# Gates in pairs of block products, heads 0 to 3's operands in the query and key tiles, and norms in three groups, in a decoder layer on one Trainium2 core

## The chip, the cores and the metric

The kernel runs on one core of a Trainium2 chip. The metric is the device time of one execution in microseconds (us); the time shown for a kernel is the median of its runs.

## The reference, cut to what matters

One decoder layer for 1,024 tokens of 1,024 channels, all in float32. A combined projection gives the attention's queries, keys and values, a pooling branch, a memory branch and three sets of gate logits, one set of 1,024 channels for each branch.

```python
h = rms_norm(x, norm_mix_pre)
q_d, k_d, v_d, u_p, q_m, gate_logits = split(h @ w_in)
a = diff_attention(q_d, k_d, v_d, lam)          # 8 heads, two softmax maps each, blocks of queries
a = rms_norm(a, subln_g) * (1.0 - lam_init)     # per head and token, over the head's 128 channels
y_attn = a @ w_attn_branch
...
gates = sigmoid(gate_logits).reshape(B, S, 3, D)
mix = gates[:, :, 0] * y_attn + gates[:, :, 1] * y_pool + gates[:, :, 2] * y_mem
x = x + rms_norm(mix @ w_out, norm_mix_post)
...                                             # then the channel mixer with its up and down products
```

The change concerns the gates of the attention branch (`gates[:, :, 0]`), the attention, its per-head norm and the product with `w_attn_branch`.

## The kernel before, in words

Products run in a split form: `split` writes a float32 tile as a high part (ScalarE, L89) and a low part (VectorE, L90), and `mm3` (L102 to L105) issues three matmuls for each product, high by high, low by high and high by low, in one accumulator of PSUM.

**Gates.** A gate tile `dt` is 128 channels by 1,024 tokens, and there are eight for the attention branch. There are two ways to compute them. `gate(dt)` is a generator that does one tile directly: 8 k-blocks by two halves of the tokens by three matmuls of 128x512, that is 48; it yields after every two k-blocks, so that its pieces can stand between other work, and stores each half from GpSimd's queue to `gate_d` in DRAM. `channels(c0)` does two tiles at once through `seven`: the operands are combined as in Strassen's scheme, with sums of weight pages and sums of the activations that were made once ahead, in seven block products in place of eight. A pair takes 84 matmuls of 128x512 and additions of the seven results on VectorE. The key and query channels go that way, and of the gates tiles 0 and 1.

**Attention.** Heads 0 to 7 run one after another, in four blocks `b` of 256 queries. For a block, `scores` puts two maps in PSUM (`pss`) and makes `z` with a maximum (VectorE) and an exponential (ScalarE); `combine` subtracts the maps with the learned lambda (VectorE, L1184); `turn_weights` transposes `z` on TensorE (`pta`) and splits it to `aT` (L89, L90); `weigh_values` multiplies with the values (`poa`, 24 matmuls of 128x256 and narrower in the last block), copies the result to `ao`, squares it, splits the square and stores `ao` to `ao_d` from GpSimd's queue; `head_norm` sums the squares with a matmul by ones (`pn`) and stores the row to `ss_d`. The steps of a block are issued several blocks apart. `weave(stages, fillers)` writes a head's steps with fillers evenly between: gates 2 and 3 in head 0, the next head's values in heads 0 to 6, its keys (`head_keys`) in heads 1 to 6, gate 4 in head 7. The order on each engine is the order in which the program issues it; `tc.issue_after` moves a step behind another one in the program. Tiles wait for the last user of the bytes that they lie on.

**Norms and merge.** Per-head norms are made in two groups of four heads: `turn_sums(g)` transposes the softmax sums (`ptn`), `load_norms(g)` loads them and the squares from DRAM in a layout with tokens on all partitions, `head_norms(g)` takes the root in small operations on VectorE, and a store puts the factors in `r_d`. Behind the attention, gates 5, 6 and 7 are issued; then for each head the attention's output `a` and its factors `rb` (broadcast to all partitions) are loaded, multiplied (L1384) and split to `ath` and `atl`. `merge_heads(dt, g)` multiplies heads `4g` to `4g + 3` with a page of `w_attn_branch` for output tile `dt`, accumulating in `pya`, and `merge(dt)` applies the gate and adds the other branches. All sixteen tiles of `ath` and `atl` lie in a pool of their own, on bytes that the attention used.

Of the kernel before, what the change touches and what calls it, by code (L numbers as in the profile page):

```python
# [41 lines left out]
def kernel(  # L42
# [818 lines left out]
    with tc.tile_pool(name="gp", reuse_waits="tile", bufs=2, side="right") as gp_:  # L861
# [163 lines left out]

        ss = gp_.tile([P, 4, H4, P], F32, tag="g", name="ss", bufs=3)
# [4 lines left out]
        ready = {2: wsplit(chunk(w_in, C_G + 2 * P), [P, KT, P])}  # L1031
        with tc.issue_after(ready[2][2].ins):
            late[0]()
# [3 lines left out]

    cstack = ExitStack()
    qkp = cstack.enter_context(tc.tile_pool(name="qkp", reuse_waits="tile", bufs=1, side="right"))
    ap_ = cstack.enter_context(tc.tile_pool(name="att", reuse_waits="tile", bufs=3, side="right"))  # L1040
    vpool = cstack.enter_context(tc.tile_pool(name="vp", reuse_waits="tile", bufs=2, side="right"))
# [163 lines left out]
    def weigh_values(h, b):  # L1205
# [10 lines left out]
        for n, ((k, qs, w, ws), i, j) in enumerate(terms):  # L1216
            nc.tensor.matmul(po[:, qs], (vh, vl)[i][:, k, :], w[j][:, ws], start=(n == 0), stop=(n == len(terms) - 1))  # L1217
# [8 lines left out]
        ends["square"] = nc.vector.tensor_tensor(out=sqs[1], in0=sq, in1=sqs[0].bitcast(F32), op=ALU.subtract)  # L1226
# [13 lines left out]
    HG = NH // 2  # L1240
    hns = {}

    def turn_sums(g):

        pt = bank((P, P), "ptn")
        nc.tensor.transpose(pt[0:HG * KT, :], sums[:, g * HG:(g + 1) * HG].rearrange("p h t -> p (h t)"), ident)
        row = ap_.tile([HG * KT, P], F32, tag="trow", name="trow", bufs=1)
        nc.scalar.activation(out=row, in_=pt[0:HG * KT, :], func=AF.Copy)
        nc.sync.dma_start(out=sum_d[g * HG:(g + 1) * HG].rearrange("h (t p) -> (h t) p", p=P), in_=row)

    def load_norms(g):

        st = small.tile([P, 4, HG, 8], F32, tag="hn", name="hn", bufs=1)
        for src, r in ((ss_d, 0), (sum_d, 3)):
            nc.sync.dma_start(out=st[:, r], in_=src[g * HG:(g + 1) * HG].rearrange("h (p f) -> p h f", f=8))
        hns[g] = st

    def head_norms(g):
# [8 lines left out]
        nc.sync.dma_start(out=r_d[g * HG:(g + 1) * HG].rearrange("h (p f) -> p h f", f=8),  # L1267
# [9 lines left out]
    first = gate(2)  # L1277
# [8 lines left out]
    with tc.issue_after(last["load"].ins):  # L1286
        ready[3] = wsplit(chunk(w_in, C_G + 3 * P), [P, KT, P])
        for dt in range(2):
            nc.sync.dma_start(out=gate_d[dt], in_=g01[dt])
    GATES = ((2, 3), (), (), (), (), (), (), (4,))  # L1290
    blocks = [(h, b) for h in range(NH) for b in range(4)]
    for h in range(NH):
        stages = []
        for b in range(4):
# [21 lines left out]
            if h == HG and b == 0:  # L1316
                stages.append(lambda: turn_sums(0))
            if h == HG and b == 1:
                stages.append(lambda: load_norms(0))
            if h == HG and b == 3:  # L1320
                def norms():
                    with tc.issue_after(last["combine"].ins):
                        head_norms(0)
                stages.append(norms)
# [8 lines left out]
        n = 0  # L1333
        for dt in GATES[h]:
            for step in steps(first if dt == 2 else gate(dt), 6 if dt == 2 else 8):
                fillers.insert(min(n, len(fillers)), step)
                n += 2
# [3 lines left out]
    turn_sums(1)  # L1341
# [3 lines left out]
    load_norms(1)  # L1345
# [5 lines left out]
    ath = [atp.tile([P, S], F32R, name="ath%d" % h) for h in range(NH)]  # L1351
    atl = [atp.tile([P, S], F32R, name="atl%d" % h) for h in range(NH)]

    pys = {}

    def merge_heads(dt, g):

        if g == 0:
            pys[dt] = wsplit(chunk(w_attn_branch, dt * P), [P, KT, P])[:2] + (bank(name="pya"), pbank(name="pya"))
        wh, wl, *py = pys[dt]  # L1360
        for i in range(2):
            hs = slice(i * H, (i + 1) * H)
            for k in range(g * HG, (g + 1) * HG):
# [52 lines left out]
    for dt in range(KT):  # L1416
        if dt >= 2:
            merge_heads(dt, 0)
# [379 lines left out]
```

## Time and profile before

| | |
|---|---|
| median of 3 runs | 1728.34 us (1728.09 to 1728.5) |
| profiled execution: its own time, as the profile's span | 1727.6 us |
| TensorE (PE) busy | 1712.8 us, 99% |
| VectorE (DVE) busy | 1241.3 us, 72% |
| ScalarE (ACT) busy | 886.6 us, 51% |
| GpSimd (POOL) busy | 45.0 us, 3% |
| gates 0 and 1 as a pair end | at about 605 us |
| head 0 | 605.8 to 642.1 us |
| heads 1 to 6 | about 33 us each |
| head 7, to the end of its last values | 839 to 882 us |

The profile is one execution; its span is the time from its first to its last instruction. Busy time is the sum of an engine's instructions; PEld is the loading of weights into TensorE, beside its matmuls. A window of the span shows the busy time of each engine in that stretch, which tells where TensorE waits. Lines like L103 are those of the kernel above.

### The profile page before, as it was taken

The numbers are of one execution on the slowest core, as the hardware profiler recorded it, in microseconds if no ns is written. First come the engines' busy times: TensorE is split into PE (matmuls) and PEld (weight loads), VectorE is DVE, ScalarE is ACT, GpSimd is POOL, SyncE is SP. The second block draws the span as 40 slices with busy tenths as digits, with TensorE's granted clock in tenths as the row PEclk, the third lists the DMA queues.
The fourth block names the chain that finished last, engine by engine and source line by source line (L and its number), as shares of the span: only waits on it lengthen the run. The fifth ranks groups of instructions, "written<-read, shape, count | busy, mean of one in ns | idle before, by whom it ended". The sixth has DMA issues, their size and how long they took to land.

```text
span 1727.6 us, 22400 instructions
## 1 busy us (share of the span) xinstructions
PE 1712.8 (99%) x8106; PEld 1421.4 (82%) x8106; DVE 1241.3 (72%) x2047; ACT 886.6 (51%) x1577; POOL 45.0 (3%) x103
## 2 busy tenths in 40 slices
PE   9999999999999999999999999999999999999998
PEld 7888888887888888888888888888888888888886
DVE  6765875666665578888866555848888888878466
ACT  5434544434544467777754344645555555543453
POOL 0000000000000011111110000000000000000000
PEclk9999999999999999999999999999999999999999
DMA  8873544444874686665556571572333423583344
GB/s 273 317 281 114 163 150 133 166 147 143 266 237 159 201 231 170 176 182 152 145 187 239 176 230 50 171 225 92 124 112 107 122 85 98 190 299 106 107 149 142
DMA packets 232803, 294.41 MB, mean 170 GB/s; under 512 B 15865, under 2 KB 161526, under 8 KB 230006
## 3 DMA queue, kind: packets, MB, share of 16 engines
q1 hardware_dynamic: 229158, 285.61, 51.8%
q0 software_dynamic: 3520, 7.38, 1.2%
q8 instruction: 64, 1.05, 0.3%
q14 instruction: 45, 0.37, 0.1%
q10 hardware_dynamic: 16, 0.00, 0.0%
HBM read 201.10 MB, written 85.56 MB: 166 GB/s over the span
## 4 chain that ended last, share of the span: by engine, by line
PE 91%; DVE 5%; DMA 2%; ACT 1%; issue 1%; SPq 0%; DVEq 0%; ACTq 0%
PE pa L103 8%; PE pa L104 8%; PE pa L105 8%; PE pb L103 5%; PE pb L104 5%; PE pb L105 5%; PE pss L1161 3%; PE poa L1217 2%; PE pd L103 2%; PE pd L105 2%; PE pd L104 2%; PE pe L105 2%; PE pe L104 2%; PE pe L103 2%; PE pout L103 2%; PE pout L105 2%
## 5 line engine op out<-in xcount | busy, mean ns | idle before, releaser
L89 ACT ACTIVATE wpage<-s 128x512 fp32r<-128x512 f32 x136 | 85.3, 627 | 108.2 <-DVE s L188 35.3
L90 DVE TENSOR_TENSOR wpage<-s,wpage 128x512 fp32r<-128x512 f32 x136 | 92.8, 688 | 43.2 <-ACT wpage L89 43.2
L1565 DVE SCALAR_TENSOR_TENSOR cvt<-gv,cols,cvt 128x1023 f32<-128x1023 f32 x88 | 112.5, 1278 | 15.6 <-ACT cvt L1561 14.9
L1165 DVE CUSTOM_DVE_ANT_0 z<-pss,hbias 128x256 f32<-128x256 f32 (+7 forms) x128 | 94.5, 752 | 26.0 <-PE pss L1161 24.8
L1170 ACT ACTIVATE z<-z,mx 128x256 f32<-128x256 f32 (+7 forms) x128 | 98.8, 773 | 20.8 <-DVE mx L1165 20.7
L103 PE MATMUL pa<-T,wpage 128*128 128x512 f32 x264 | 102.8, 389 | 0.0
L105 PE MATMUL pa<-T,wpage 128*128 128x512 f32 x264 | 102.7, 389 | 0.0
L104 PE MATMUL pa<-T,wpage 128*128 128x512 f32 x264 | 102.7, 389 | 0.0
L1161 PE MATMUL pss<-ks,q 128*128 128x512 f32 (+5 forms) x384 | 86.6, 349 | 1.4 <-DVE mx L1165 1.4
L89 ACT ACTIVATE page<-blk 128x1024 fp32r<-128x1024 f32 (+1 forms) x42 | 41.4, 989 | 85.7 <-PE pe L104 50.6
L90 DVE TENSOR_TENSOR page<-blk,page 128x1024 fp32r<-128x1024 f32 (+1 forms) x42 | 47.5, 1130 | 38.1 <-ACT page L89 38.1
L1161 PEld LDWEIGHTS pss<-ks,q 128*128 128x128 f32 x384 | 62.9, 189 | 11.1 <-DVE mx L1165 6.2
L103 PE MATMUL pd<-page 128*128 128x512 f32 x176 | 68.7, 390 | 0.0
L104 PE MATMUL pd<-page 128*128 128x512 f32 x176 | 68.5, 389 | 0.0
L105 PE MATMUL pd<-page 128*128 128x512 f32 x176 | 68.3, 389 | 0.0
L103 PE MATMUL pa<-hT,wpage 128*128 128x512 f32 x168 | 65.5, 390 | 0.1
L105 PE MATMUL pa<-hT,wpage 128*128 128x512 f32 x168 | 65.4, 389 | 0.0
L104 PE MATMUL pa<-hT,wpage 128*128 128x512 f32 x168 | 65.4, 389 | 0.0
L1217 PEld LDWEIGHTS poa<-aT,v 128*128 128x128 f32 x480 | 60.7, 190 | 3.0 <-ACT srow L1237 1.4
L1217 PE MATMUL poa<-aT,v 128*128 128x256 f32 (+1 forms) x480 | 62.5, 280 | 0.0
L103 PEld LDWEIGHTS pa<-T,wpage 128*128 128x128 f32 x264 | 49.6, 188 | 10.7 <-DVE gv L250 0.3
L104 PEld LDWEIGHTS pa<-T,wpage 128*128 128x128 f32 x264 | 49.6, 188 | 10.2
(429 smaller groups left out, 4965.7 us busy)
## 6 DMA issues: line engine op xcount, KB each, us to landing
q<-q_d SPq DMA_DIRECT2D x64, 256.0 KB, 5.1
wd<-in_w_down_dram SPq DMA_DIRECT2D x22, 512.0 KB, 5.0
tw_d<-wd SPq DMA_DIRECT2D x11, 1024.0 KB
rawv<-in_w_up_dram SPq DMA_DIRECT2D x22, 512.0 KB, 5.8
rawu<-in_w_up_dram SPq DMA_DIRECT2D x22, 512.0 KB, 4.1
ff_d<-cvt SPq DMA_DIRECT2D x22, 512.0 KB, 5.4
blk<-ff_d SPq DMA_DIRECT2D x20, 512.0 KB, 7.9
br<-tw_d SPq DMA_DIRECT2D x20, 512.0 KB, 5.0
```

The costliest lines, as they stand in the source:

```text
L89: copy = nc.scalar.activation(out=hi, in_=src, func=AF.Copy)
L90: nc.vector.tensor_tensor(out=lo, in0=src, in1=hi.bitcast(F32), op=ALU.subtract)
L103: nc.tensor.matmul(o, ah, bh, start=first, stop=False, skip_group_check=onto)
L104: nc.tensor.matmul(o, ah, bl, start=False, stop=False, skip_group_check=onto)
L105: return nc.tensor.matmul(o, al, bh, start=False, stop=last, skip_group_check=onto)
L1161: last["scores"] = nc.tensor.matmul(pss[:, i * H:i * H + m], q[:, j, c, ts], keys, start=(j == 0), stop=(j == 1))
L1165: nc.vector.tensor_tensor_reduce(out=halves(z[:, 0:n]), in0=pss.rearrange("p (a m) -> p a m", a=2)[:, 0:parts, 0:m], in1=halves(biases[h][ ...
L1170: nc.scalar.activation(out=z[:, 0:n], in_=z[:, 0:n], func=AF.Exp, scale=-1.0, bias=mx[:, c:c + 1], accum_out=sm if c else sums[:, h, t:t + 1])
L1217: nc.tensor.matmul(po[:, qs], (vh, vl)[i][:, k, :], w[j][:, ws], start=(n == 0), stop=(n == len(terms) - 1))
L1565: nc.vector.scalar_tensor_tensor(out=cv[:, sh:], in0=u[:, 0:S - sh], scalar=w, in1=cv[:, sh:], op0=ALU.mult, op1=ALU.add)
```

## The change

Gates 2 and 3, and 4 and 5, become two more pairs by `channels` ahead of the pair 0 and 1; each pair is stored with one DMA of 1 MB from SP's queue. Gate 6 is head 0's filler and gate 7 head 7's, with six of its eight steps between the head's stages and two behind them; no gate is issued behind the attention. Norms are made in three groups, heads 0 to 3, 4 to 6 and 7; the second group's transposes, loads and roots are issued in head 7. The sums' row is stored from ScalarE's queue. The subtraction that makes the low part of the square goes from VectorE to GpSimd, but for the last two blocks of head 7, and the store of `ao` is issued behind it.

The operands of the merge become tiles `at`: those of heads 0 and 1 lie in the four key tiles, those of heads 2 and 3 in the two query tiles, the others in the pool as before. For this the query and key pool stays open until the merge is over, and the pool of values is opened ahead of the attention's. The merge runs in pairs: `merge_heads(d, ks)` multiplies the heads `ks` for output tiles `2d` and `2d + 1`, with pages of weights for four heads by two tiles (`merge_weights`); tiles 4 to 7 go one at a time through `merge_one`. Loads of the first four heads' `a` and `rb` are issued together, ahead of the loads for the last norm group.

TensorE's order at the end of the attention, before: the last transposes of `z` (`pta`) stand among the matmuls of gate 5 (`pg`, which is issued later in the program but moved up to behind the scores), and so do the row sums (`pn`) and the last values (`poa`).

```order
L1200 MATMUL pta<-ident,z 128x128 x7
L105 MATMUL pg_8570<-hTh_110,wl 128x512
L103 MATMUL pg_8570<-hTh_110,wh 128x512
L104 MATMUL pg_8570<-hTl_112,wh 128x512
L105 MATMUL pg_8570<-hTh_110,wl 128x512
L103 MATMUL pg_8570<-hTh_110,wh 128x512
L1246 MATMUL ptn<-ident,sums 32x128
```

and behind the last values, where gate matmuls surround the sums of the last squares:

```order
L1217 MATMUL poa<-aT_8475,v 128x256
L103 MATMUL pg_8570<-hTh_110,wh 128x512
L104 MATMUL pg_8570<-hTl_112,wh 128x512
L105 MATMUL pg_8570<-hTh_110,wl 128x512
L103 MATMUL pg_8570<-hTh_110,wh 128x512
L104 MATMUL pg_8570<-hTl_112,wh 128x512
L105 MATMUL pg_8570<-hTh_110,wl 128x512
L1235 MATMUL pn<-sq_8524,ones 128x256
L103 MATMUL pg_8598<-hTh_111,wh 128x512
L1235 MATMUL pn<-sq_8525,ones 128x256
```

After the change the same two places read so on TensorE (`pya` is the merge of head 0, `at` its operand):

```order
L1205 MATMUL pta<-ident,z 128x128 x7
L1254 MATMUL ptn<-ident,sums 8x128
L1240 MATMUL pn<-sq_8636,ones 128x256
L1240 MATMUL pn<-sq_8637,ones 128x256
L1222 MATMUL poa<-aT_8650,v 128x256
```

```order
L1222 MATMUL poa<-aT_8678,v 128x256
L1222 MATMUL poa<-aT_8677,v 128x256
L1240 MATMUL pn<-sq_8746,ones 128x256
L1240 MATMUL pn<-sq_8747,ones 128x256
L103 MATMUL pya<-at_8762,wh 128x512 x2
L104 MATMUL pya<-at_8763,wh 128x512
L105 MATMUL pya<-at_8762,wl 128x512
```

The gates that stood between these steps are gone from here, and the merge of head 0 follows the last `pn` directly.

In the first half of head 0, the scores (`pss`) of TensorE stood between matmuls of gate 3 before:

```order
L1161 MATMUL pss_4963<-ks_4881,q 128x384 x2
L1161 MATMUL pss_4969<-ks_4882,q 128x384 x2
L103 MATMUL pg_4889<-hTh_110,wh 128x512
L104 MATMUL pg_4889<-hTl_112,wh 128x512
L105 MATMUL pg_4889<-hTh_110,wl 128x512
L103 MATMUL pg_4889<-hTh_110,wh 128x512
L104 MATMUL pg_4889<-hTl_112,wh 128x512
L105 MATMUL pg_4889<-hTh_110,wl 128x512
L1200 MATMUL pta<-ident,z 128x128 x3
L1161 MATMUL pss_5000<-ks_4881,q 128x512 x2
```

and are followed after the change by the transposes at once:

```order
L1166 MATMUL pss_5209<-ks_5135,q 128x384 x2
L1166 MATMUL pss_5215<-ks_5136,q 128x384 x2
L1205 MATMUL pta<-ident,z 128x128 x3
L1166 MATMUL pss_5238<-ks_5135,q 128x512 x2
L1222 MATMUL poa<-aT_5226,v 128x256
```

One filler of six matmuls is gone at this place. On SP's queue behind the attention (`a` and `rb` are the loads of a head, `hn` those of a norm group, `r_d` the factors' store) the order was:

```order
L1255 DMA hn_8534<-sum_d_105 128x4x8
L1255 DMA hn_8534<-ss_d_104 128x4x8
L1381 DMA a_8750<-ao_d_94 128x1024
L1383 DMA rb_8752<-r_d_106 128x1024
L1381 DMA a_8757<-ao_d_94 128x1024
L1383 DMA rb_8759<-r_d_106 128x1024
```

and is now, with the last group's loads behind the first four heads:

```order
L1277 DMA r_d_106<-hn_8410 128x3x8
L1416 DMA a_8777<-ao_d_94 128x1024
L1418 DMA rb_8779<-r_d_106 128x1024
L1416 DMA a_8781<-ao_d_94 128x1024
L1418 DMA rb_8783<-r_d_106 128x1024
L1416 DMA a_8785<-ao_d_94 128x1024
L1418 DMA rb_8787<-r_d_106 128x1024
L1416 DMA a_8789<-ao_d_94 128x1024
L1418 DMA rb_8791<-r_d_106 128x1024
L1265 DMA hn_8793<-ss_d_104 128x8
```

The four heads' loads moved ahead of a norm group's, and the second group's store stands ahead of them. The core of the diff:

```diff
+        for dt in (2, 4):
+            g = channels(C_G + dt * P)
+            nc.sync.dma_start(out=gate_d[dt:dt + 2].rearrange("e p s -> p e s"), in_=g)
...
-        ready = {2: wsplit(chunk(w_in, C_G + 2 * P), [P, KT, P])}
+        ready = {6: wsplit(chunk(w_in, C_G + 6 * P), [P, KT, P])}
...
         ao = ap_.tile([P, 2 * P], F32, tag="ao", name="ao", bufs=2)
         nc.scalar.activation(out=ao, in_=po, func=AF.Copy)
-        nc.gpsimd.dma_start(out=ao_d[h][:, bs], in_=ao)
...
-        ends["square"] = nc.vector.tensor_tensor(out=sqs[1], in0=sq, in1=sqs[0].bitcast(F32), op=ALU.subtract)
+        engine = nc.vector if h == NH - 1 and b >= 2 else nc.gpsimd
+        ends["square"] = engine.tensor_tensor(out=sqs[1], in0=sq, in1=sqs[0].bitcast(F32), op=ALU.subtract)
+        nc.gpsimd.dma_start(out=ao_d[h][:, bs], in_=ao)
...
+    GROUPS = (slice(0, HG), slice(HG, NH - 1), slice(NH - 1, NH))
...
-        nc.sync.dma_start(out=sum_d[g * HG:(g + 1) * HG].rearrange("h (t p) -> (h t) p", p=P), in_=row)
+        nc.scalar.dma_start(out=sum_d[hs].rearrange("h (t p) -> (h t) p", p=P), in_=row[0:n])
...
+            with tc.issue_after(marks["head"].ins) if g == 2 else nullcontext():
+                nc.sync.dma_start(out=st[:, r], in_=src[hs].rearrange("h (p f) -> p h f", f=8))
...
-        ready[3] = wsplit(chunk(w_in, C_G + 3 * P), [P, KT, P])
...
-    GATES = ((2, 3), (), (), (), (), (), (), (4,))
...
+        if h == 0:
+            for n, step in enumerate(steps(first, 6)):
+                fillers.insert(min(2 * n, len(fillers)), step)
+        if h == NH - 1:
+            tail = steps(gate(7), 8)
+            fillers, tail = fillers + tail[:6], tail[6:]
         weave(stages, fillers)
...
+    merge_weights(0, 0)
+    for step in tail:
+        step()
+    turn_sums(2)
     head_norm(*blocks[-2])
     weigh_values(*blocks[-1])
     head_norm(*blocks[-1])
-    load_norms(1)
     cstack.close()
...
+    at = [qkp.tile([P, 2, S], F32R, tag="q", name="at%d" % h, bufs=2) if h in (2, 3) else
+          [qkp.tile([P, S], F32R, tag="ks%d%d" % (c, h), name="at%d%d" % (c, h)) for c in range(2)] if h < 2 else
+          atp.tile([P, 2, S], F32R, name="at%d" % h) for h in range(NH)]
...
-        for dt in range(5, KT):
-            for step in steps(gate(dt), 8):
-                step()
...
+        for h in range(HG):
+            load_head(h)
+        load_norms(2)
+        for h in range(2):
+            normed_head(h)
+        merge_heads(0, range(2))
+        merge_weights(1, 0)
+        for h in range(2, HG):
+            normed_head(h)
+        merge_heads(0, range(2, HG))
+        merge_heads(1, range(HG))
+        merge_weights(0, 1)
+        with tc.issue_after(ends["square"].ins):
+            head_norms(2)
+        for h in range(HG, NH):
+            load_head(h)
+            normed_head(h)
+        merge_heads(0, range(HG, NH))
+        merge_weights(1, 1)
...
+    for dt in range(2):
+        merge(dt)
+    merge_heads(1, range(HG, NH))
+    for dt in range(2, 4):
+        merge(dt)
+    for dt in range(4, KT):
+        merge_one(dt)
         merge(dt)
```

More of the change, by code (lines that the diff above doesn't have):

```diff
@@ L1276 @@
     load_keys(0)
-    first = gate(2)
+    first = gate(6)
     head_bias(0)
@@ L1315, with norms @@
                 stages.append(lambda n=n: weigh_values(*blocks[n - 1]))
[L1316 to L1324, printed above, removed]
+            if h in (HG, NH - 1):
+                g = h // (NH - 1)
+                if b == 0:
+                    stages.append(lambda g=g: turn_sums(g))
+                if b == 1:
+                    stages.append(lambda g=g: load_norms(g))
+                if b == 3 - g:
+                    def norms(g=g):
+                        with tc.issue_after(last["combine"].ins):
+                            head_norms(g)
+                    stages.append(norms)
             if b in (1, 3) and h + 1 < NH:
@@ L1369, with load_head @@
                                 op0=ALU.mult)
-        for dt in range(5, KT):
-            for step in steps(gate(dt), 8):
-                step()
-        for h in range(NH):
-            if h == HG:
-                with tc.issue_after(ends["square"].ins):
-                    head_norms(1)
-                for dt in range(2):
-                    merge_heads(dt, 0)
+        heads = {}
+        def load_head(h):
             a = sub.tile([P, S], F32, tag="a", name="a")
```

88 lines of the change are left out of this document (55 added, 33 removed).

## The prediction

> **What bounds the kernel now.** I read the page's head first, then busy time by stage in windows of the span, then the rows of the timeline around head 0 and behind the last head, and last the grouped rows and transfers.
>
> ```profile
> span 1727.6 us, 22400 instructions
> PE 1712.8 (99%) x8106; PEld 1421.4 (82%) x8106; DVE 1241.3 (72%) x2047; ACT 886.6 (51%) x1577; POOL 45.0 (3%) x103
> PE 91%; DVE 5%; DMA 2%; ACT 1%; issue 1%; SPq 0%; DVEq 0%; ACTq 0%
> ```
>
> PE is busy for all but 14.8 us. So a matmul removed is time saved only if PE finds other work, and a new wait of PE is paid in full. The windows below give busy us of PE, PEld, DVE, ACT, POOL, then clock, DMA share and GB/s: gate and query pairs (550 to 600), head 0 (605.8 to 642.1), heads 1 and 2, head 7 (839 to 871.5), its end, and what follows the attention (882 to 924).
>
> ```profile
> 550.00:600.00 50.00, 50.00 (x222) 41.41 (x221) 26.85 (x38) 19.93 (x31) 2.81 (x3) 1.00 0.59 188
> 605.80:642.10 36.30, 35.42 (x194) 30.39 (x194) 26.00 (x66) 23.05 (x55) 4.46 (x8) 1.00 0.80 219
> 642.10:675.00 32.90, 32.86 (x204) 28.46 (x203) 26.61 (x70) 23.71 (x59) 4.25 (x8) 1.00 0.67 196
> 675.00:708.00 33.00, 32.42 (x203) 28.33 (x203) 28.96 (x75) 26.28 (x66) 4.70 (x9) 1.00 0.61 163
> 839.00:871.50 32.50, 31.33 (x189) 26.84 (x187) 28.01 (x69) 24.55 (x59) 4.25 (x8) 1.00 0.33 93
> 871.50:882.00 10.50, 10.50 (x67) 8.50 (x65) 5.69 (x9) 5.14 (x14) 1.61 (x3) 1.00 0.33 92
> 882.00:924.00 42.00, 42.00 (x187) 34.54 (x186) 26.49 (x37) 18.55 (x24) 4.32 (x8) 1.00 0.82 295
> ```
>
> A head needs about 33 us of PE and 26 to 29 of DVE. The next rows count the gates' matmuls alone in head 0, head 7 and its end: they cover the attention's chain of softmax steps, and behind 882 they cover the loading of the normed heads.
>
> ```profile
> 605.80:642.10 36.30, 21.77 (x84) 15.24 (x84) 0.00 (x0) 1.90 (x4) 1.00 0.80 219
> 839.00:871.50 32.50, 12.65 (x45) 8.08 (x46) 0.00 (x0) 0.60 (x1) 1.00 0.33 93
> 871.50:882.00 10.50, 6.22 (x23) 3.90 (x23) 0.00 (x0) 0.60 (x1) 1.00 0.33 92
> ```
>
> **Pairs of block products.** Two gates took 96 matmuls of 128x512, a pair takes 84; two new pairs save 24. The pitch, from twelve gate matmuls up to the first scores:
>
> ```profile
> 602.60 0.39 PE L103 MATMUL pg<-hTh,wh 128*128 128x512 f32 x1
> 605.32 0.56 PE L1161 MATMUL pss<-ks,q 128*128 128x128 f32 x4
> ```
>
> (605.32 − 602.60)/12 = 0.2267 us, times 24 = **−5.4**. The pairs' additions lie on DVE in a stage where it is busy 26.85 of 50; the two stores of 1 MB go out there at a DMA share of 0.59; both cost nothing as long as PE's 50.00 of 50 holds. If that cover is gone, DVE would have to rise by 23 us per 50.
>
> **Head 0** loses gate 3, 48 matmuls or 10.9 us. PE keeps 35.42 − 10.9 = 24.5. DVE loses one split of a page (1.23, row at 873.38 below) and three subtractions of 0.42 to POOL: 26.00 − 2.5 = 23.5. The best share of DVE that any head shows is 28.96/33 = 0.88, so the head takes 23.5/0.88 = 26.7. Without loss it would take 36.3 − 10.9 = 25.4. So the least is near 0.3 (DVE at 0.91) and DVE's share says 1.3; if each of the four blocks shows both waits of the rows below (0.5 each, which the gates cover now), it is 4. I take **+2.0**, between the two.
>
> ```profile
> PE pss L1161 <- DVE mx L1165: 1.4, 4, 0.5
> PE pta L1200 <- DVE z L1184: 1.3, 3, 0.6
> ```
>
> **Head 7 up to its last transposes.** There were 68 gate matmuls (45 + 23), now one gate of 48: −20 × 0.2267 = −4.5, so of 41.83 busy in 839 to 882 PE keeps 37.3. DVE has 28.01 + 5.69 = 33.7; it gains the 16 small operations of the second norm group and loses two subtractions: 33.7 + 16 × 0.19 − 0.8 = 35.9, at 0.88 is 40.8. Against 43 − 4.5 = 38.5 that is 2.3 over; half the gate still lies under the last blocks, so I take **+1.5** (0 to 4).
>
> ```profile
> L153 DVE SCALAR_TENSOR_TENSOR hn<-hn x6: 182/186/193, 774.9 to 894.8; 128x32 f32<-128x32 f32 x6
> 875.93 0.93 PE L1200 MATMUL pta<-ident,z 128*128 128x128 f32 x7
> 878.93 3.00 PE L1217 MATMUL poa<-aT,v 128*128 128x256 f32 x24
> ```
>
> **Behind the last transposes, T0 = 876.9.** Now three gates (882 to 924, PE 42.00 of 42) cover the tail; after the change none does. By the order, SP's load `a` of head 0 overwrites bytes of the last `z`, so it waits for T0, and `rb` goes with it; head 1's `rb` waits for the end of the last `poa`. PE has only `ptn`, four `pn` and `poa` until the merge of head 0, some 0.35 + 2.84 + 0.68 = 3.9 us. How a pair of loads became an operand before:
>
> ```profile
> 883.59 0.39 PE L1235 MATMUL pn<-sq,ones 128*128 128x256 f32 x1
> 887.38 0.45 SPq L1381 DMA_DIRECT2D a<-ao_d  x1
> 887.87 0.42 SPq L1383 DMA_DIRECT2D rb<-r_d  x1
> 893.64 1.28 DVE L1384 SCALAR_TENSOR_TENSOR a<-a,gs,rb 128x1024 f32<-128x1024 f32 x1 [0.40 <-DMA rb<-r_d]
> 894.96 1.06 ACT L89 ACTIVATE ath<-a 128x1024 fp32r<-128x1024 f32 x1 [4.39 <-DVE a L1384]
> 896.05 1.23 DVE L90 TENSOR_TENSOR atl<-a,ath 128x1024 fp32r<-128x1024 f32 x1 [0.57 <-ACT ath L89]
> 873.38 1.23 DVE L90 TENSOR_TENSOR wl<-raw,wh 128x1024 fp32r<-128x1024 f32 x1
> 877.20 1.16 DVE L90 TENSOR_TENSOR aT<-pta,aT 128x512 fp32r<-128x512 f32 x2 [1.05 <-ACT aT L89]
> ```
>
> From `rb`'s issue to the multiplication 893.64 − 887.87 = 5.77, from there to the low part 897.28 − 893.64 = 3.64. With 0.45 for `a`'s issue, head 0 is ready at T0 + 9.9. PE's 3.9 us of work lie before that: it idles 6.0, in pieces (for `aT`, for the square, for head 0). Head 1's `rb` is issued at about T0 + 4.7, its operand is there at T0 + 13.5, PE is free at 12.3 after head 0's 12 matmuls: +1.1. For heads 2 and 3 DVE and ACT need 3.6 − 0.2 per head against 12 × 0.2267 = 2.72: +0.65 and +0.6 (an estimate from these rows). Sum **+8.3**. The ends: transfers of 512 KB alone and the median beside other traffic:
>
> ```profile
> raw<-in_w_attn_branch_dram SPq DMA_DIRECT2D x8, 512.0 KB, 4.2
> rb<-r_d SPq DMA_DIRECT2D x8, 512.0 KB, 9.0
> ```
>
> 4.2 in place of 5.77 makes it 6.7, and 4.5 if heads 2 and 3 keep up as well; 9.0 makes it 11. I take 5.77, since it is the same pair in the same place. Later heads lie behind four heads of d = 1, 48 matmuls or 10.9 us, which cover 4 × 3.6 less what DVE did already, and the pages of weights; without that cover each head costs 0.9.
>
> The page "DMA: Bandwidth & Descriptors" of the Trainium skill, "Anatomy of one DMA — SWDGE (gpsimd) path", fits 2.0 us plus the bytes over 436 GB/s, for the pair of 1 MB an estimate of 4.4 us; the sum would then be 1.4 lower. These are SP's queue, not that path, and the row has 5.77.
>
> **Heads 1 to 6: the square's subtraction on POOL.** 6 × 4 × 0.42 = 10 us leave DVE, but PE is busy 32.42 of 33.00 and 32.86 of 32.90 there, so 0.04 to 0.58 a head is to be had at most. POOL's price isn't in the trace: its nearest row scales to 1.61 × 256/1152 = 0.36, and is 1.6 unscaled.
>
> ```profile
> L1047 POOL TENSOR_SCALAR_AFFINE_SELECT bias<-bias 128x1152 f32<-128x1152 f32 x1 | 1.6, 1612 | 0.0
> 883.11 0.42 DVE L1226 TENSOR_TENSOR sq<-sq,sq 128x256 fp32r<-128x256 f32 x1 [4.75 <-ACT sq L1225]
> ```
>
> `pn` uses the square two blocks (16 us) later, so either price hides; the store of `ao` queued behind it is read after the attention. I take **−0.5** (−2.2 to +0.5). The third group of norms adds one transpose (0.3 of PE, in the tail's 3.9); its sums' store moves from SP to ACT's queue, one issue.
>
> **Sum.** −5.4 + 2.0 + 1.5 + 8.3 − 0.5 = +5.9: 1727.6 + 5.9 = 1733.5. The median of the runs stands 0.7 above the profile's span, so **1734**.
>
> **Rivals.**
> - *No change*: the pairs of loads land in 4.2 and DVE keeps up: tail 4.5 to 5, head 0 and 7 lose together 1 to 2. −5.4 + 4.7 + 1.5 − 0.5 = +0.3: 1728.6. For it: DVE is free behind T0. Against it: `rb`'s median of 9.0.
> - *Faster*: the loads aren't what PE waits for in the tail. If `a` and `rb` are there when the last `pn` ends, only the waits for `aT` (its split ended at 878.36, 1.5 behind T0) and for the square's low part (883.53, 1.6 behind the last `poa`) stay: 3.1, less a little for the small matmuls between them, 3.0 in place of 8.3. With heads 0 and 7 at their lower ends and the relief at −1.0, −5.4 + 3.0 − 1.0 = −3.4: 1724.9. It decides once the tail costs under 3.0. For it: PE's order holds the chain's steps without gates between. Against it: T0 + 0.45 + 4.2 + 3.6 is 8.3, later than PE's 3.9 + 3.0.
> - *The clock falls*: the tail's waits join to one that is long enough. The trace shows that PE's clock follows idling:
>
> ```profile
> 1720.72 0.39 PE L105 MATMUL pd<-page 128*128 128x512 f32 x1
> 1724.00:1725.00 1.00, 0.00 (x0) 0.00 (x0) 0.60 (x1) 0.00 (x0) 0.00 (x0) 0.78 0.20 76
> 1725.00:1726.00 1.00, 0.00 (x0) 0.00 (x0) 0.00 (x0) 0.00 (x0) 0.00 (x0) 0.50 1.03 383
> ```
>
> The granted clock falls to 0.50 some 3.4 to 4 us after the last matmul at 1721.1. My longest wait is about 2 us; with `rb` at 9.0 it is 5. Then the tail is 11, and 3.4 us of matmuls run at half clock, +1.7: 1733.5 + 2.7 + 1.7 + 0.7 = 1738.6.
>
> "TensorE: Matmul & The Clock Gate", Part "HAM oscillation — how this bites in real kernels", of the Trainium skill says the same: no gaps of PE above some 3.4 us, or the next matmuls start at half clock; the trace's end agrees, at 3.4 to 4 us.
>
> **How the numbers follow.** A difference under 0.2% (3.5 us, 1724.9 to 1731.8) is about what can't be told from none. My forecast has 0.50, the clock 0.08 (slower together 0.58); no change 0.25; faster 0.17. The range from 1724.5 to 1740 leaves out half of the faster case and the clock's end with a median load in every head.
>
> **What the changed profile would show.** PE idle in the 12 us behind the last transposes, 6 to 9 us in all, ended by `at`'s splits on ACT and DVE at the first `pya`; the windows of head 0 near 27 us with PE under 92% busy and DVE near 88%; head 7 with PE idle 1 to 2; POOL with rows for `sq`; 8,037 PE instructions less what the trace drops; the granted clock 1.00 in the tail. I am wrong if head 0's operand comes within 7 us of T0, if head 0 runs at PE's 24.5, or if the new pairs of gates don't run at 0.2267 a matmul.

## The result, and the profile after

The changed kernel takes 1739.84 us (median of 4 runs, 1738.93 to 1740.38), the kernel before 1728.42 beside it: 1.0062 times as long, with an interval of 1.0047 to 1.0076. So it is slower by 11.4 us, where I had forecast 5.7. It lies 0.2 us below the upper end of the range that I gave. The page of its profile, in the lines that answer to the first ones shown of before:

```profile
span 1737.1 us, 22410 instructions
PE 1715.5 (99%) x8083; PEld 1417.5 (82%) x8083; DVE 1247.4 (72%) x2057; ACT 891.3 (51%) x1588; POOL 63.9 (4%) x125
PE 85%; DVE 7%; DMA 3%; issue 2%; ACT 2%; SPq 1%; POOL 0%; DVEq 0%; POOLq 0%
```

PE has 24 gate matmuls less, one transpose more (8083 instructions in place of 8106), and is busy 2.7 us longer: that cannot be read from idle time alone. To find the place, both spans are cut at the same points of the work: first scores, ScalarE's copy of the last output of heads 1 and 6, end of the last transposes, end of the last values, first matmul of the merge, first matmul of the output product (head 0's last output parts the first stretch in two). Columns as before: length, busy us of PE, PEld, DVE, ACT, POOL, clock, DMA share, GB/s. Before:

```profile
605.32:651.37 46.05, 45.13 (x259) 38.73 (x258) 31.07 (x84) 27.80 (x69) 5.51 (x10) 1.00 0.77 216
651.37:684.63 33.26, 32.68 (x205) 28.72 (x204) 29.90 (x79) 26.06 (x65) 4.27 (x8) 1.00 0.63 175
684.63:848.40 163.77, 161.22 (x996) 139.65 (x995) 142.67 (x375) 125.74 (x307) 21.38 (x40) 1.00 0.65 175
848.40:876.86 28.46, 28.46 (x167) 24.32 (x166) 24.03 (x52) 21.00 (x47) 4.84 (x9) 1.00 0.19 59
876.86:881.93 5.07, 5.07 (x35) 4.26 (x35) 1.16 (x2) 1.32 (x4) 0.51 (x1) 1.00 0.38 97
881.93:910.81 28.88, 28.88 (x128) 23.64 (x128) 16.78 (x29) 11.04 (x16) 3.78 (x7) 1.00 0.81 287
910.81:997.85 87.04, 87.04 (x385) 72.07 (x384) 50.69 (x62) 35.24 (x47) 0.54 (x1) 1.00 0.62 208
```

After:

```profile
641.34:678.20 36.86, 34.04 (x200) 27.95 (x199) 30.32 (x87) 26.92 (x71) 6.71 (x11) 1.00 0.96 258
678.20:712.71 34.51, 34.36 (x210) 29.61 (x209) 25.02 (x61) 24.25 (x57) 7.39 (x12) 1.00 0.63 184
712.71:878.39 165.68, 162.84 (x1001) 140.08 (x1000) 140.80 (x364) 127.69 (x311) 36.84 (x60) 1.00 0.62 170
878.39:905.88 27.49, 27.33 (x157) 21.82 (x155) 23.33 (x61) 20.14 (x47) 6.89 (x12) 1.00 0.11 31
905.88:910.76 4.88, 3.60 (x28) 3.21 (x27) 1.16 (x2) 1.17 (x4) 0.84 (x2) 1.00 0.79 270
910.76:914.89 4.13, 0.78 (x3) 0.37 (x2) 1.79 (x4) 2.50 (x5) 1.07 (x2) 0.90 0.80 243
914.89:1007.20 92.31, 91.16 (x384) 73.42 (x385) 62.05 (x87) 39.04 (x51) 0.00 (x0) 0.97 0.73 247
```

With the gate matmuls that left each stretch, counted in the traces and priced at 0.2267 us:

| stretch | before | after | gate matmuls | their time | lost |
|---|---|---|---|---|---|
| heads 0 and 1 | 79.31 | 71.37 | −48 | −10.9 | 2.9 |
| heads 2 to 6 | 163.77 | 165.68 | −1 | −0.2 | 2.1 |
| head 7, to the last transposes | 28.46 | 27.49 | −11 | −2.5 | 1.5 |
| to the end of the last values | 5.07 | 4.88 | −7 | −1.6 | 1.4 |
| to the merge | 28.88 | 4.13 | −125 | −28.3 | 3.6 |
| merge, 384 matmuls | 87.04 | 92.31 | 0 | 0 | 5.3 |

The losses sum to 16.8; less the 5.4 of the 24 matmuls that are 11.4, as measured. (The spans differ by 9.5 only, since the profiled execution of before reached the attention 2.1 later than the changed kernel's, less its 168 more matmuls: 605.32 against 641.34 − 38.09 = 603.25.) The tail of the changed kernel in its timeline:

```profile
905.91 0.33 SPq L1416 DMA_DIRECT2D a<-ao_d  x1
906.34 0.38 SPq L1418 DMA_DIRECT2D rb<-r_d  x1
...
910.80 0.32 SPq L1418 DMA_DIRECT2D rb<-r_d  x1
...
911.97 0.84 PE L1240 MATMUL pn<-sq,ones 128*128 128x256 f32 x2 [1.20 <-ACT sq L1228]
...
912.47 1.28 DVE L1423 SCALAR_TENSOR_TENSOR a<-a,gs,rb 128x1024 f32<-128x1024 f32 x1
...
914.89 1.22 PE L103 MATMUL pya<-at,wh 128*128 128x512 f32 x2 [2.09 <-ACT at L89]
...
918.15 1.28 DVE L1423 SCALAR_TENSOR_TENSOR a<-a,gs,rb 128x1024 f32<-128x1024 f32 x1 [2.05 <-DMA rb<-r_d]
...
921.84 0.50 PE L104 MATMUL pya<-at,wh 128*128 128x512 f32 x1 [0.64 <-DVE at L90]
```

Head 0's loads go at the last transposes (905.88), its multiplication runs at 912.47, and PE waits for its high part until 914.89. Head 1's factors are issued when the last values end, and hold VectorE until 918.15.

### The profile page after: what moved, and what is told of

It is laid out like the page before. It is cut to its first block, busy times and chain, and to the rows that moved or that the text cites. A ratio compares the mean times of both kernels' runs of the same rounds, so it can differ in the third digit from the quotient of the medians.

```text
span 1737.1 us, 22410 instructions
## 1 busy us (share of the span) xinstructions
PE 1715.5 (99%) x8083; PEld 1417.5 (82%) x8083; DVE 1247.4 (72%) x2057; ACT 891.3 (51%) x1588; POOL 63.9 (4%) x125
## 4 chain that ended last, share of the span: by engine, by line
PE 85%; DVE 7%; DMA 3%; issue 2%; ACT 2%; SPq 1%; POOL 0%; DVEq 0%; POOLq 0%
PE pa L103 9%; PE pa L105 9%; PE pa L104 9%; PE pb L103 6%; PE pb L104 6%; PE pb L105 6%; PE pd L103 2%; PE pd L104 2%; PE pd L105 2%; DVE z L1170 2%; PE poa L1222 2%; PE pe L104 2%; PE pe L103 2%; PE pe L105 2%; PE pout L105 2%
## 5 line engine op out<-in xcount | busy, mean ns | idle before, releaser
L89 ACT ACTIVATE wpage<-s 128x512 fp32r<-128x512 f32 x144 | 90.3, 627 | 116.0 <-DVE s L188 46.1
L90 DVE TENSOR_TENSOR wpage<-s,wpage 128x512 fp32r<-128x512 f32 x144 | 98.1, 688 | 47.6 <-ACT wpage L89 47.5
L103 PE MATMUL pa<-hT,wpage 128*128 128x512 f32 x192 | 74.8, 390 | 0.0
L105 PE MATMUL pa<-hT,wpage 128*128 128x512 f32 x192 | 74.7, 389 | 0.0
L104 PE MATMUL pa<-hT,wpage 128*128 128x512 f32 x192 | 74.7, 389 | 0.0
L105 PEld LDWEIGHTS pa<-T,wpage 128*128 128x128 f32 x264 | 49.6, 188 | 10.3
```

Of the source, the lines that this page charges most:

```text
L89: copy = nc.scalar.activation(out=hi, in_=src, func=AF.Copy)
L90: nc.vector.tensor_tensor(out=lo, in0=src, in1=hi.bitcast(F32), op=ALU.subtract)
L103: nc.tensor.matmul(o, ah, bh, start=first, stop=False, skip_group_check=onto)
L104: nc.tensor.matmul(o, ah, bl, start=False, stop=False, skip_group_check=onto)
L105: return nc.tensor.matmul(o, al, bh, start=False, stop=last, skip_group_check=onto)
```

## The experiments

In each, the stretches of the table are compared; where a kernel has the same order in a stretch, they agree within some hundredths (head 0 takes 36.86, 36.87, 36.87 in three kernels), so they tell more than the medians, which move by 1 to 2 us. The merge is less steady, since it waits for transfers: head 1's factors take from 5.5 to 7.4 us in kernels with the same order there.

**The square on VectorE again.**

```diff
-        engine = nc.vector if h == NH - 1 and b >= 2 else nc.gpsimd
+        engine = nc.vector
```

> The changed kernel with one edit: the low part of every square is made on VectorE again. The trace of the changed kernel has GpSimd's subtraction at 0.746 us where VectorE's took 0.42, and heads 2 to 6 came out 1.4 us longer than before, while I had forecast 0.5 shorter. Theory A (the move to GpSimd lengthens the heads: its row stands between ScalarE's square and the store of ao): heads 2 to 6 lose the 1.4 again, the median goes from 1739.8 to about 1738.5. Theory B (the heads are longer because the steps stand elsewhere, not because of the square; VectorE's 12 us were hidden work): no change, 1739.8, within 1. If VectorE was the limit in heads 0 and 7, as I forecast, they get longer by 1 to 2 with the square on it: 1741.

1737.42 us (before 1729.07 beside it; 1.0048, 1.0033 to 1.0063). Heads 0 and 1 take 71.54 (71.37), heads 2 to 6 164.72 (165.68), head 7 26.76 (27.49): 1.5 less in all, theory A's size. Head 0 alone takes 0.3 more with VectorE's share back, and head 7 takes 0.7 less, where VectorE as the limit would have cost 1 to 2; so its busy time isn't what limited them. The merge takes 90.40 (92.31), with head 1's factors there 1.9 sooner, though their load is issued at the same point (4.9 behind the last transposes) and the edit doesn't touch it. The row of the changed kernel's subtraction on GpSimd:

```profile
L1230 POOL TENSOR_TENSOR sq<-sq,sq 128x256 fp32r<-128x256 f32 x30 | 22.4, 746 | 4.8 <-ACT sq L1228 4.2
```

**Keeping the clock.** Seventeen unused transposes in the waits of the tail.

```diff
+    keep(5, ends["poa"])
     head_norm(*blocks[-1])
+    keep(12, ends["pn"])
```

`keep(n, mark)` issues `n` transposes of the identity behind `mark`: five behind the last values, twelve behind the last row sums.

> The changed kernel with 17 transposes of the identity added on TensorE, 5 behind the last values and 12 behind the last row sums, where it waits for head 0's operand; their result isn't used. In the changed kernel TensorE does little from 910.8 to 914.9 and the granted clock is 0.50 from 914 to 920.9. Theory A (the low activity halves the clock, and this costs half of 6.9 us): the clock stays at 1.00 there, the wait for head 0 stays, and the median falls by 3.4 to about 1736.4. Theory B (the slow matmuls there are slow since the loads and splits share the memory with them): the matmuls stay at 0.43 us apart, no change. If the added transposes end later than head 0's operand, some tenths come back.

1739.29 us (1.0060, 1.0043 to 1.0076). The clock is 1.00 and the matmuls 0.23 apart, so theory A has the cause of the slow matmuls; but its 3.4 us don't come. The merge takes 91.66 in place of 92.31. The timeline of this run says where they went:

```profile
918.12 1.28 DVE L1432 SCALAR_TENSOR_TENSOR a<-a,gs,rb 128x1024 f32<-128x1024 f32 x1 [1.44 <-DMA rb<-r_d]
...
920.55 0.50 PE L103 MATMUL pya<-at,wh 128*128 128x512 f32 x1 [1.24 <-ACT at L89]
...
921.80 0.50 PE L104 MATMUL pya<-at,wh 128*128 128x512 f32 x1 [0.76 <-DVE at L90]
```

Head 0's matmuls are done by 919.3 and PE waits 1.24 and 0.76 for head 1, whose multiplication starts at 918.12, as late as in the changed kernel (918.15). There, at half clock, head 0's matmuls took most of that time.

**The gate's end behind the last values.** The last 12 matmuls of gate 7 go there.

```diff
     merge_weights(0, 0)
-    for step in tail:
-        step()
     turn_sums(2)
     head_norm(*blocks[-2])
     weigh_values(*blocks[-1])
+    last["scores"] = ends["poa"]
+    for step in tail:
+        step()
     head_norm(*blocks[-1])
```

> The changed kernel, with the last two steps of gate 7 (12 matmuls of 128x512, 2.7 us) issued behind the last values instead of ahead of the last transposes. Theory A (the tail lacks cover, and its waits of 1.2 and 2.1 and the clock at half are the price): the waits shrink by 2.7, the clock stays at 1.00 (3.4), and head 7 ahead of them gets 2.7 less work, of which it saves 1.5 to 2.7: in all about 5 us, 1735. Theory B (head 7 is bound by VectorE and its chain, so that it doesn't get shorter by the matmuls taken out): only the clock's 3.4 and what the gap took, at most 1736.5; if head 7 then waits more than before, 1738.

1741.47 us (1.0070, 1.0055 to 1.0085), slower than either theory had. With 12 matmuls less, head 7 takes 28.13 to its last transposes (27.49): its end is a chain from `z` over the transposes and ScalarE's and VectorE's split, and these matmuls were not its length. The 0.64 more are the clock's: it fell at 905.4, and the last seven transposes take 1.76 at 0.50 in place of 1.14. The last values come 6.38 after (4.88), at half clock too.

**Heads 0 and 1 early.** Their loads go to the query tiles, which are free, and their multiplication ahead of the last square.

```diff
+    early = [qkp.tile([P, 2, S], F32, tag="q", name="ar%d" % h, bufs=2) for h in range(2)]
+    for h in range(2):
+        nc.sync.dma_start(out=early[h][:, 0], in_=ao_d[h])
+        nc.sync.dma_start(out=early[h][:, 1], in_=r_d[h:h + 1, :].partition_broadcast(P))
...
+            ends["turn"] = nc.vector.scalar_tensor_tensor(out=early[h][:, 0], in0=early[h][:, 0], scalar=gs, in1=early[h][:, 1],
```

> The changed kernel, with heads 0 and 1's attention output and factors loaded to the two query tiles, which are free before the last transposes, multiplied and split behind the last aT split, so ahead of the last square; their operands stay in the key tiles. Theory A (head 0's operand comes late because its loads wait for the bytes of the last z and its multiplication stands behind the last square on VectorE): the wait of 2.1 for head 0 goes, the clock stays at 1.00 (3.4), and the next wait is for head 2: in all 5 to 6 us less, 1734 to 1735. Theory B (VectorE and ScalarE need 3.6 us a head anyway and are the limit behind the attention): the wait moves to heads 1 and 2 and only 1 to 2 us are gained, 1738; with the clock still falling there, 1739.

1738.82 us (1.0059, 1.0044 to 1.0074), theory B's figure. The wait for head 0 is gone (the merge starts as the last values end), but those now run at half clock (6.43 us in place of 4.88), and the merge takes 91.85. From head 6's last output to the output product it is 3.2 shorter than the changed kernel. What kept the merge long came out only later: its matmuls were 0.2333 apart.

**One pair less, the gates back as cover.** Gates 4 and 5 in head 0, 6 in head 7, 7 behind the last values.

```diff
-        for dt in (2, 4):
+        for dt in (2,):
...
-            for n, step in enumerate(steps(first, 6)):
+            for n, step in enumerate(steps(first, 6) + steps(gate(5), 8)):
...
-            fillers, tail = fillers + tail[:6], tail[6:]
+            fillers, tail = fillers + steps(gate(6), 8) + tail[:1], tail[1:]
...
     weigh_values(*blocks[-1])
+    last["scores"] = ends["poa"]
+    for step in tail:
+        step()
```

> The changed kernel with only one new pair of gates, tiles 2 and 3: gates 4 and 5 are fillers of head 0, gate 6 of head 7, and gate 7 (but for its first six matmuls) is issued behind the last values. Norm groups, operand tiles, merge order and GpSimd's square stay as changed. TensorE has 12 matmuls more than in the changed kernel, +2.7 us. Theory A (the losses are missing cover for VectorE's and the loads' chains: 3 us in heads 0 and 1, 1.5 in head 7, 1.4 and 9.1 behind it): the segment to the last output of head 1 comes back to the time before but for 0.3, the wait for head 0's operand and the low clock go, and the median is 1739.8 + 2.7 - 3 - 9 to 10 = 1730. Theory B (the operands in the query and key tiles, the merge in pairs or the queues cost it, whatever cover there is): the tail stays 5 us or more longer than TensorE's work, 1736 or more.

1739.64 us (1.0065, 1.0053 to 1.0077). Heads 0 and 1 take 78.62 against 79.31 before, with the same gate matmuls in them: their loss was missing cover, and is gone. The rest of theory A fails. Head 7 takes 31.12 to its last transposes: the last gate matmul ahead of them starts at 893.73, 5 us before they end, and PE is busy 10.84 of the last 13.78 us. The tail trips over ScalarE's order:

```profile
913.26 0.60 ACT L1135 ACTIVATE g<-pg 128x512 f32<-128x512 f32 x1 [4.84 <-PE pg L105]
...
914.01 1.04 ACT L89 ACTIVATE at<-a 128x1024 fp32r<-128x1024 f32 x1
...
915.09 1.22 DVE L90 TENSOR_TENSOR at<-a,at 128x1024 fp32r<-128x1024 f32 x1 [8.42 <-ACT at L89]
```

Head 0 had been multiplied at 906.67 and its high part stands behind the copy of the gate that was to cover it. Cover works only if nothing that it covers is queued behind it.

**The same with the square on VectorE.**

> The last run's kernel with every square's low part on VectorE again. With the square on VectorE the changed kernel's heads 0 to 7 came out 1.5 us shorter. Theory A (GpSimd's 0.75 us per square stand in the chain of a head): 1 to 1.5 less than that run, about 1728.5, even with before or below it. Theory B (where gates cover the heads, a square that takes 0.3 longer is hidden): no difference to that run, within 0.7.

1737.83 us (1.0060, 1.0048 to 1.0072), 1.8 less than the last. Heads 0 and 1 take 79.29 in place of 78.62, heads 2 to 6 163.23 in place of 165.93, and 163.77 before. Behind them the last values take 7.42 in place of 4.89, with the clock at 0.50. TensorE's order is that of before, matmul by matmul, until head 4; with the square on GpSimd it differs from the end of head 1 on. So either GpSimd's 0.746 us or the order that goes with it costs 2.7 us in heads 2 to 6, 2.0 with heads 0 and 1; which of the two wasn't separated.

**Gate 7 in head 0.**

```diff
-            for n, step in enumerate(steps(first, 6)):
+            for n, step in enumerate(steps(first, 6) + steps(gate(7), 8)):
...
-            tail = steps(gate(7), 8)
-            fillers, tail = fillers + tail[:6], tail[6:]
+            tail = []
```

> The changed kernel with gate 7 as a second filler of head 0, behind gate 6; head 7 has no filler and nothing is in the tail. Theory A (heads 0 and 1 lost 3 us for want of gate 3's matmuls as cover): with 48 matmuls (10.9 us) more in head 0, the segment to the last output of head 1 grows by 10.9 - 2.9 = 8 us. Theory B (heads 0 and 1 are longer for another reason, for instance the square or the values' place): it grows by 10.9. For head 7: if the chain of scores, VectorE, ScalarE and transposes sets its time, taking 48 matmuls out shortens it by no more than 5 us from the last output of head 6 to the last transposes (27.5 now); if TensorE does, by 10.9. Median by A with the chain: 1739.8 - 3 + 6 = 1743.

1746.67 us (1.0104, 1.0089 to 1.0119). Heads 0 and 1 take 78.55: 7.2 more for 10.9 us of matmuls, so 3.7 of these were free, as theory A had it. Head 7 has no gate at all and takes 27.34 to its last transposes (27.49 with 41 gate matmuls, 9.3 us): PE's work isn't what sets it. The median is 3.7 above that theory's 1743: with no gate in head 7 or behind it the clock falls three times from 903.9 on, and the last values take 7.48 in place of 4.88.

**All pieces for two pairs.** The early loads, the square on VectorE, six unused transposes behind the last ones, head 2's multiplication ahead of head 1's low part.

> The changed kernel with both new pairs, the early load of heads 0 and 1, the square on VectorE, six unused transposes of the identity behind the last transposes of z, and head 2's multiplication ahead of head 1's low part on VectorE. Theory A (each of these took one piece of the tail: the square 1.5 in the heads, the early load 3, the clock at half under the last values 1.5, the order on VectorE 1.3): 1738.8 - 1.5 - 1.5 - 1.3 = 1734.5. Theory B (they are one chain, so that what one gives up the next takes): 1737. In both it stays above before, since the heads 0, 1 and 7 keep their loss of about 5.

1737.67 us (1.0056, 1.0043 to 1.0070). The heads are 1.2 shorter, the clock is 1.00, the last values take 4.89; the merge still takes 92.10. The figure is near theory B's 1737, but the runs with four bytes below show another reason for it.

**One pair with early loads.** As the one-pair kernel with the square on VectorE, with the early loads and VectorE's order of the last run, and with gate 7 issued so that its matmuls may stand between the last transposes.

> One new pair of gates (tiles 2 and 3), gates 4 and 5 in head 0, gate 6 in head 7, the square on VectorE, heads 0 and 1 loaded early to the query tiles, and gate 7 issued so that its matmuls may stand between the last transposes, as gate 5's did before, and behind the last values. In the last one-pair runs heads 0 to 6 took the time of before, but the gate's matmuls stood behind the last values alone, so head 7 had no cover at its end (31.1 us from head 6's last output to the last transposes, before 28.5), and ScalarE split head 0 only behind the gate's copy. Theory A (cover at the right places is all that the tail lacks): 28.5 again to the last transposes, 5.0 to the last values, the merge within 2 us of its 87.0, clock 1.00, and the 12 matmuls saved against before show: 1728.2 - 2.7 + 1 to 2 = 1727. Theory B (the merge in pairs and the load of heads in two lots cost time by themselves): the stretch behind the last values stays 4 to 5 us too long, 1731.

1731.43 us (1.0019, 1.0010 to 1.0028). The last values come 5.13 after the transposes, PE waits for nothing in the merge, and that takes 89.60 in place of 87.04, from its first matmul to its last. 384 × 0.2333 = 89.6. The three kernels with early loads have this pitch and no other kernel has; they share a new tile, the 4 bytes per partition of `gs` in the pool of small tiles, and every pool that is opened later on that side of the memory starts behind it.

**Four bytes.** The changed kernel with such a tile that nobody reads; the two kernels above with `gs` in spare bytes of an old tile instead.

```diff
+    nc.gpsimd.memset(small.tile([P, 1], F32, tag="gs", name="gs0", bufs=1), 0.0)
```

```diff
+    shared = const.tile([P, 17], F32, name="epsilon")
+    epsilon = shared[:, 0:1]
...
-    gs = small.tile([P, 1], F32, tag="gs", name="gs", bufs=1)
+    gs = shared[:, 1:2]
```

The tile `epsilon` was that large before, and one column of it was used.

> The changed kernel with one tile of 4 bytes per partition added to the pool of small tiles, written once and never read; every engine's order stays as it was but for that one write. Theory A (places of the tiles set the pitch): the pitch goes to 0.2333 in the merge and 0.230 from 180 to 300 us, and the median rises by 4 to 5 us, 1744. Theory B (the order or transfers): no change, 1739.8.

> The run with both new pairs, early loads of heads 0 and 1, square on VectorE and the changed order on VectorE, with the scale column in the same spare bytes. Theory A (places of the tiles): the pitch of the merge 0.2267, 5 us less than that run, 1732.5, which leaves the missing cover of heads 0 and 1 (3.1) and of head 7's end as the change's price. Theory B: 1737.5 again.

> The last run's kernel, with its scale column kept in spare bytes of an old tile, so that no tile is added and every other tile stands where it stood in the changed kernel. In the last run the pitch of matmuls was 0.2333 us in the merge and about 0.230 from 180 to 300 us and in the output product, where the changed kernel has 0.2267; no wait shows there. Theory A (the added tile of 4 bytes moved the operands' places in the memory, and that is the slower pitch): 0.2267 again, the merge 87.1, and 2.5 + 1.4 + 1.5 us less: 1726, below before by 2. Theory B (the pitch comes from the order of the work or from transfers beside it): no change, 1731.

1744.69 us (1.0096, 1.0083 to 1.0110), 1731.75 us (1.0022, 1.0012 to 1.0032) and 1726.44 us (0.9987, 0.9978 to 0.9996), against 1728.22: theory A in all three. With both pairs that kernel stays 3.5 us above before: heads 0 and 1 take 71.57 and keep their loss of 3.1, and of the 11.8 us that the changed kernel loses from head 6's last output to the output product 6.0 stay (122.38 against 149.45 before with 146 gate matmuls more), 2.7 of them waits for operands in the merge. Five matmuls of the merge with the four bytes, and in the changed kernel:

```profile
939.80 0.40 PE L105 MATMUL pya<-at,wl 128*128 128x512 f32 x1
...
940.97 0.40 PE L104 MATMUL pya<-at,wh 128*128 128x512 f32 x1
```

```profile
939.66 0.39 PE L105 MATMUL pya<-at,wl 128*128 128x512 f32 x1
...
940.79 0.39 PE L104 MATMUL pya<-at,wh 128*128 128x512 f32 x1
```

1.17 us against 1.13, at a granted clock of 1.00 in both. The same shows some 700 us earlier, in a stretch where PE is busy throughout and the transfers are alike; with the four bytes, then in the changed kernel:

```profile
180.00:300.00 120.00, 120.00 (x524) 97.82 (x523) 82.63 (x126) 58.00 (x95) 0.00 (x0) 1.00 0.44 141
180.00:300.00 120.00, 120.00 (x530) 99.00 (x529) 83.85 (x128) 58.35 (x97) 0.00 (x0) 1.00 0.44 141
```

The last kernel beats before and after: its stretches, to be held against the two lists above, show heads as before, no gap of PE behind the last transposes, and the merge at 87.04.

```profile
624.20:670.14 45.94, 44.87 (x259) 38.73 (x258) 31.10 (x84) 27.82 (x69) 5.50 (x10) 1.00 0.85 242
670.14:703.41 33.27, 32.70 (x205) 28.71 (x204) 29.90 (x79) 26.07 (x66) 4.27 (x8) 1.00 0.63 175
703.41:866.60 163.19, 160.95 (x996) 139.62 (x995) 142.71 (x375) 125.67 (x308) 21.39 (x40) 1.00 0.65 175
866.60:897.52 30.92, 30.60 (x176) 25.96 (x175) 25.77 (x68) 21.19 (x48) 4.84 (x9) 1.00 0.33 104
897.52:902.66 5.14, 5.14 (x36) 4.49 (x36) 3.67 (x5) 2.87 (x6) 1.04 (x2) 1.00 0.63 222
902.66:907.74 5.08, 5.08 (x23) 3.94 (x23) 3.85 (x4) 2.39 (x5) 1.07 (x2) 1.00 0.74 271
907.74:994.78 87.04, 87.04 (x385) 72.07 (x384) 57.11 (x83) 39.62 (x52) 0.56 (x1) 1.00 0.71 239
```

It has 12 matmuls less than before (2.7 us) and gains 1.8.

## Why the prediction was right in sign and half in size

- **Pairs, −5.4: right.** The pairs run at 19.04 us each, 84 × 0.2267, with PE busy throughout.
- **Head 0, +2.0: right that missing cover costs it, short in size: 2.9.** The loss reaches into head 1. Heads 0 and 1 with two gates as cover take the time of before in all four kernels with one pair (78.6 to 79.3). My measure, VectorE's busy share of 0.88 as a ceiling, was wrong: VectorE is busy 30.32 of 36.86, and giving it the square back changes heads 0 and 1 by 0.2. What counts is the chain of each block: PE waits 1.9 us for the scores' maximum in heads 0 and 1, 0.3 before.
- **Head 7, +1.5: measured 1.5**, in part by luck, as 0.7 of it goes with the square (27.49 against 26.76). There is a slip in it: 19 gate matmuls left up to the end of the last values, not 20 (one stood in both of my windows), 11 of them from head 6's last output to the last transposes. The runs show a firmer statement than mine: with 41, 29 or no gate matmuls it takes 27.5, 28.1, 27.3, and the 28.1 has its last transposes at half clock.
- **The square on GpSimd, −0.5: wrong in sign**; the heads lost 1.5 to it (1.0 in heads 2 to 6, 0.7 in head 7, −0.2 in heads 0 and 1). The step that failed is "either price hides". The price, 0.746, lay inside my bounds of 0.36 and 1.6, but the row sums don't use the square two blocks (16 us) later: a row of the working has a `pn` at 883.59, 0.06 behind the subtraction's end, and in four heads of the changed kernel the sum runs as the subtraction ends:

```profile
714.00 0.75 POOL L1230 TENSOR_TENSOR sq<-sq,sq 128x256 fp32r<-128x256 f32 x1
...
714.73 0.46 PE L1240 MATMUL pn<-sq,ones 128*128 128x256 f32 x2
```

These two matmuls take 0.39 with the square on VectorE, so the wait itself is some 0.07 a head, an estimate from these two rows. I had also left out the order on TensorE that goes with the move, which differs from the end of head 1 on. The rest of the loss in heads 2 to 6, 1.1 of 2.1, is explained by no run; the one-pair kernels with the square on VectorE don't have it (163.2).

- **The tail, +8.3: measured 1.4 + 3.6 + 5.3 = 10.3.** Up to the merge it lost 5.0, where I had 6.0; in the merge 5.3, where I had 2.3. Head 0's low part was forecast for 9.9 after the last transposes and came at 10.2 (916.09). The term that was mis-sized is head 1's. I put its operand at 13.5, where the working's own rows give 4.7 + 5.77 + 3.64 = 14.1; and its factors' transfer, put at 5.77, took 7.35 from 910.80 to 918.15, beside the other heads' loads (317 GB/s from 914 to 917.5, a row below), so that the operand came at 15.9. The transfer isn't the same each time: it took 5.47, 6.21 and 6.74 in the runs with the square on VectorE, the four bytes and the kept clock. With 5.47 the loss behind the last transposes is 8.4, so how near +8.3 came depends on the execution that was profiled.
- **The clock, a rival at 0.08: it came, and cost next to nothing in this kernel** (1739.29 with it kept, 1739.84 without). I had made it hang on one wait of 3.4 us; the longest was 2.09. And I had added its slow matmuls to the sum, where they fill a wait for head 1. Where they fill none they cost about what I added (1.7): the last values take 6.43 in place of 4.88 with early heads.
- **TensorE's instructions**: 8,037 was a slip; 8106 less 24 and one transpose more are the 8083 of the profile.

## What to carry to other kernels

Before work that covers a chain is made cheaper or moved, measure the chain without it: matmuls that stand between dependent steps save less than their own time when they leave (7.9 of 10.9 us in heads 0 and 1, 1.0 of 2.5 in head 7). Put the cover where nothing of the chain is queued behind it on any engine, and load what is needed first into space that is free before the chain ends. Cut two profiles at the same points of the work and price the moved instructions: that gives each stage's loss to a few tenths where idle time and medians don't, save for stages that wait for transfers.

## What the runs showed of the hardware

The clock follows what TensorE does in a window, not one gap. It was halved for 3.41 us or two or three times that (10.24 in the one-pair kernel with the square on VectorE), so the stretch of 3.41 us ahead of each fall is taken to hold the cause. The changed kernel, then the run with early heads, then the run with the square on VectorE:

```profile
910.63:914.04 3.41, 0.91 (x4) 0.37 (x2) 1.77 (x3) 1.70 (x5) 1.07 (x2) 1.00 0.82 260
914.04:917.45 3.41, 2.52 (x5) 1.61 (x6) 1.22 (x1) 0.80 (x1) 0.00 (x0) 0.50 0.93 317
```

```profile
905.97:909.38 3.41, 2.12 (x13) 1.27 (x12) 2.63 (x5) 1.84 (x4) 0.54 (x1) 1.00 0.34 90
909.38:912.79 3.41, 3.41 (x19) 3.41 (x18) 2.29 (x3) 1.43 (x2) 0.51 (x1) 0.50 0.99 367
```

```profile
907.62:911.03 3.41, 2.16 (x16) 1.76 (x15) 0.46 (x2) 1.07 (x3) 0.71 (x2) 1.00 0.85 332
911.03:914.44 3.41, 1.12 (x3) 0.48 (x3) 2.25 (x3) 1.43 (x2) 0.51 (x1) 1.00 0.98 246
```

PE was busy 0.91, 2.12 and 1.12 us ahead of the three falls, and 2.16 in a window that no fall followed; ahead of the second fall no wait was longer than 0.93. But busy time alone doesn't decide it. In the run with two pairs and the old places PE was busy 1.72 us of such a stretch (its place is counted back in steps of 3.413 us from the clock's fall at the kernel's end), and the clock stayed at 1.00:

```profile
918.09:921.50 3.41, 1.72 (x8) 1.10 (x6) 2.25 (x8) 0.00 (x0) 0.00 (x0) 1.00 0.72 238
921.50:924.91 3.41, 3.25 (x14) 2.71 (x15) 2.13 (x8) 1.06 (x1) 0.00 (x0) 1.00 1.00 361
```

Its matmuls are all of 128x512, where the stretch with 2.12 has mostly transposes and sums of squares; whether that is the difference, no run shows. "TensorE: Matmul & The Clock Gate" of the Trainium skill, "What's actually happening" in Part 1, has a free-running window of 3413 ns, which these lengths agree with; its section "HAM oscillation — how this bites in real kernels" warns of idle gaps above some 3.4 us, and here the clock fell without one.

A tile of 4 bytes per partition that nobody reads changes the pitch of matmuls elsewhere: 0.2333 in place of 0.2267 us in the merge, and 0.230 in place of 0.227 from 180 to 300 us and in the output product, in all 4.9 us over the changed kernel. Since nothing but one write was added to the program, the places of the other tiles are what differs. Which operand and which boundary it is, and how far the tiles moved, wasn't tried.
